# First products ahead of the second block's transposes, and roots by GpSimd's power operation

## The chip, the cores and the metric

The kernel runs on one core of one Trainium2 chip. The metric is the device time of one execution in microseconds (us). The engines are PE (TensorE, the matrix unit), DVE (VectorE), ACT (ScalarE), POOL (GpSimd) and SP (SyncE, which here only issues DMAs). Each engine works through its own queue in order: an instruction that waits for another engine holds all that stand behind it on its own engine.

## The reference, cut to what matters

The program computes one layer of a hybrid block for 16 learned meta tokens and 2048 tokens (T = 2064) of 1024 f32 values. What this change touches is the first product, `p`, and the norm ahead of it:

```python
def rms_norm(x, g):
    xf = x.astype(jnp.float32)
    y = xf * lax.rsqrt(jnp.mean(xf * xf, axis=-1, keepdims=True) + EPS)
    return (y * g.astype(jnp.float32)).astype(x.dtype)
...
h = jnp.concatenate([meta, x], axis=1)
p = rms_norm(h, norm_mix_pre[l]) @ w_in[l]
...
oa = rg_lru_group(xa, ya, ...)          # a recurrence over the tokens
ob = forgetting_attention_group(...)    # 8 heads with a forget gate
oc, v_own = rwkv7_group(pc, ...)        # a recurrence over the tokens
mixed = jnp.concatenate([oa, ob, oc], axis=-1) @ w_out[l]
h = h + rms_norm(mixed, norm_mix_post[l])
...
f = causal_dwconv(rms_norm(h, norm_ffn_pre[l]) @ ffn_up[l], ffn_conv[l])
f = (jax.nn.gelu(gate, approximate=True) * val) @ ffn_down[l]
h = h + rms_norm(f, norm_ffn_post[l])
```

The inputs of `oa`, `ob` and `oc` are columns of `p`.

## The kernel before, in words

**Number format.** The large products run on pairs: a value is split into a high and a low half, ACT copies the high half, DVE subtracts it from the value for the low one, and a product is three matmuls (high by high, low by high, high by low; L181 to L183).

**Stages.** The first stage is the input projection, with the two recurrences running beside it; attention, the output projection and the two feed-forward products follow. The change is in the first stage. It takes the tokens in thirds (`part` 0, 1, 2) of two blocks each (`w_in_tokens`): 400 tokens (the meta tokens and three tiles of 128) and 384, then 384 and 384, then 256 and 256.

**Tokens.** For each tile `w_in_norm` calls `norm_transpose`. SP loads the tile `xt` into one of four buffers `nt_x` (L131). ACT squares it and sums (L123). DVE makes the reciprocal root from the sum, by three small operations and three Newton steps of two (`rstd_from`, L98 and L99), and scales the tile by root and gain (L136). PE transposes it in eight pieces into two PSUM tiles `pst` (L149). ACT copies the high half `xh` (L155), and DVE makes the low half `xl` (L156). The transposes of all tiles of a third, of both blocks, are written ahead of that third's products.

**Products.** `w_in_part` is a generator. It begins with the forget gate's columns (`w_in_gate`: 16 matmuls a block, L300 and L301, into `psf`; ACT and DVE bring the result to `fo`, and SP stores it to DRAM as `scr_f`, L306). Then come 24 units of 128 columns each; a unit is 24 matmuls for each block, into `psp`. In the first third `w_in_weights` loads a unit's raw weights into a buffer of the token tiles (`nt_x`, L171), splits them on ACT (L175) and DVE (L176) into `wh` and `wl`, and stores both halves to DRAM for the other thirds, which only read them back.

**What stands around it.** Between the tokens and the first products, DVE zeroes a tile and POOL issues 12 DMAs of it into the padding of `scr_p` (L2202 to L2204). After the gate and the first 12 units (READY = 13, the gate counted as one) come the constants: attention's masks (`attn_consts`), those of the recurrences (`rwkv_consts`, `lru_consts`), and columns of parameters that PE transposes (L911, `pscol`). Then the recurrences run as generators beside the rest of the products. The forget gate's own chain (`gate_block`, L411 to L429) is one of their parts: SP reads `scr_f` back, and ACT and DVE take its logarithm and sums.

**What sets the order.** The program's text is not yet the order in the queues. A scheduler runs the program on a modelled timeline and deals the instructions to the engines' queues, with a priority by their place in the text; a changed text or a changed modelled duration deals what follows anew. `issue_after(x)` makes the instructions inside it wait for x, so that they aren't put early.

Names of the recurrence that will be met: `rps` are its PSUM tiles, L1203 its first products, L1252 (L1298 in the changed kernel) the matmuls of a small triangular solve, in which PE, ACT and DVE take turns; `rwitmp` (L1222, then L1268) are small products of that solve on POOL.

## Time and profile before

| What | Before |
|---|---|
| Median of 3 runs | 2978.02 us (2972.48, 2978.02, 2979.31) |
| The profiled execution's own time | 2974.88 us |
| Its span, first to last instruction | 2973.2 us |
| PE busy | 2840.2 us, 96% of the span |
| DVE, ACT, POOL busy | 2015.4, 1505.3, 1281.3 us |

The page cuts the span into 40 equal slices of 74 us and gives each engine's busy share in tenths, and under PEclk the TensorE clock that was granted, in tenths of full speed:

```profile
PE   6999999999978889999999999999999999999998
DVE  5257654675678766556756988888778787646766
POOL 1001121131214566766722667455655444656443
PEclk9999899999989899999999999999999999999999
```

PE is full but for the first slice and those around 850 us, where the first stage ends. In the clock's row the fifth slice (297 to 372 us) shows 8: there lies the passage from the first third to the second. The passage to the last third lies around 600 us, in the eighth and ninth, where the clock stays at 9 or more.

### The profile page before, as it was taken

The numbers are of one execution on the slowest core, as the hardware profiler recorded it, in microseconds if no ns is written. First come the engines' busy times: TensorE is split into PE (matmuls) and PEld (weight loads), VectorE is DVE, ScalarE is ACT, GpSimd is POOL, SyncE is SP. The second block draws the span as 40 slices with busy tenths as digits, with TensorE's granted clock in tenths as the row PEclk, the third lists the DMA queues.
The fourth block names the chain that finished last, engine by engine and source line by source line (L and its number), as shares of the span: only waits on it lengthen the run. The fifth ranks groups of instructions, "written<-read, shape, count | busy, mean of one in ns | idle before, by whom it ended". The sixth has DMA issues, their size and how long they took to land.

```text
span 2973.2 us, 53343 instructions
## 1 busy us (share of the span) xinstructions
PE 2840.2 (96%) x18854; PEld 2448.6 (82%) x18854; DVE 2015.4 (68%) x3974; ACT 1505.3 (51%) x2937; POOL 1281.3 (43%) x1555
## 2 busy tenths in 40 slices
PE   6999999999978889999999999999999999999998
PEld 6998899889865555566568999999999999787887
DVE  5257654675678766556756988888778787646766
ACT  4246432444346555445635665666575665324333
POOL 1001121131214566766722667455655444656443
PEclk9999899999989899999999999999999999999999
DMA  6776479576654257535245665577777774436453
GB/s 219 235 233 223 156 246 322 171 240 213 209 127 95 70 130 215 125 95 130 72 133 187 204 191 173 167 230 211 205 212 219 218 199 131 155 114 222 148 171 121
DMA packets 470344, 530.52 MB, mean 178 GB/s; under 512 B 86862, under 2 KB 356888, under 8 KB 468524
## 3 DMA queue, kind: packets, MB, share of 16 engines
q1 hardware_dynamic: 469308, 526.18, 58.4%
q8 instruction: 148, 2.42, 0.3%
q14 instruction: 120, 0.98, 0.1%
q0 software_dynamic: 768, 0.93, 0.1%
HBM read 368.07 MB, written 158.90 MB: 177 GB/s over the span
## 4 chain that ended last, share of the span: by engine, by line
PE 72%; DVE 8%; DMA 7%; ACT 5%; POOL 4%; issue 3%; SPq 1%; DVEq 0%; POOLq 0%; ACTq 0%
PE psu L181 9%; PE psu L182 9%; PE psu L183 9%; PE psp L183 5%; PE psp L182 5%; PE psp L181 5%; PE psd L181 4%; PE psd L182 4%; PE psd L183 4%; PE po L733 3%; PE sc L710 2%; PE pswo L181 2%; PE pswo L182 2%; PE pswo L183 2%; PE mx L581 2%
## 5 line engine op out<-in xcount | busy, mean ns | idle before, releaser
L182 PE MATMUL psu<-xo,uw 128*128 128x344 f32 x1848 | 591.5, 320 | 0.0
L181 PE MATMUL psu<-xo,uw 128*128 128x344 f32 x1848 | 586.0, 322 | 3.5 <-DVE vb L1907 2.1
L183 PE MATMUL psu<-xo,uw 128*128 128x344 f32 x1848 | 581.9, 320 | 0.3 <-DVE uw L1716 0.3
L181 PE MATMUL psp<-xh,wh 128*128 128x384 f32 (+2 forms) x1152 | 378.3, 328 | 0.1
L183 PE MATMUL psp<-xh,wl 128*128 128x384 f32 (+2 forms) x1152 | 377.0, 328 | 0.7 <-DMA wl<-scr_wk 0.7
L182 PE MATMUL psp<-xl,wh 128*128 128x384 f32 (+2 forms) x1152 | 377.6, 328 | 0.0
L1716 DVE TENSOR_TENSOR uw<-uq,uw 128x512 fp32r<-128x512 f32 x341 | 318.8, 940 | 61.3 <-ACT uw L1715 58.3
L181 PEld LDWEIGHTS psu<-xo,uw 128*128 128x128 f32 x1848 | 345.8, 188 | 5.1 <-DVE vb L1907 3.1
L182 PEld LDWEIGHTS psu<-xo,uw 128*128 128x128 f32 x1848 | 347.2, 188 | 0.0
L183 PEld LDWEIGHTS psu<-xo,uw 128*128 128x128 f32 x1848 | 345.7, 188 | 1.1 <-DVE uw L1716 1.1
L1715 ACT ACTIVATE uw<-uq 128x512 fp32r<-128x512 f32 x462 | 288.1, 627 | 100.1 <-PE psu L183 47.3
L715 ACT ACTIVATE p<-sc,bias 128x512 f32<-128x512 f32 (+4 forms) x352 | 196.4, 590 | 166.8 <-PE sc L711 141.9
L586 DVE TENSOR_REDUCE mc<-mx 128x1 f32<-128x512 f32 (+5 forms) x352 | 191.8, 566 | 119.4 <-PE mx L581 82.9
L1855 DVE SCALAR_TENSOR_TENSOR uy<-psu,ffn_cols,uy 128x342 f32<-128x342 f32 (+1 forms) x390 | 220.6, 567 | 62.4 <-ACT uy L1853 60.7
L1716 POOL TENSOR_TENSOR uw<-uq,uw 128x512 fp32r<-128x512 f32 x121 | 184.1, 1521 | 136.7 <-ACT uw L1715 112.9
L1863 POOL TENSOR_TENSOR uy<-uy,uy 128x342 f32<-128x342 f32 (+1 forms) x132 | 144.2, 1092 | 228.7 <-DVE uy L1855 63.1
L183 PEld LDWEIGHTS psp<-xh,wl 128*128 128x128 f32 x1152 | 219.9, 191 | 7.1 <-issue 4.6
L181 PEld LDWEIGHTS psp<-xh,wh 128*128 128x128 f32 x1152 | 219.8, 191 | 4.5 <-issue 2.6
L182 PEld LDWEIGHTS psp<-xl,wh 128*128 128x128 f32 x1152 | 220.0, 191 | 3.7 <-issue 2.3
L754 POOL TENSOR_TENSOR acc<-acc,p 128x512 f32<-128x512 f32 (+3 forms) x186 | 196.5, 1059 | 48.5 <-DVE acc L754 21.4
L1716 DVE TENSOR_TENSOR fo<-u,fo 128x896 fp32r<-128x896 f32 x88 | 100.3, 1140 | 133.0 <-ACT fo L1715 132.4
L1715 ACT ACTIVATE fo<-u 128x896 fp32r<-128x896 f32 x88 | 81.2, 923 | 207.6 <-PE psd L183 122.3
(489 smaller groups left out, 6301.5 us busy)
## 6 DMA issues: line engine op xcount, KB each, us to landing
uq<-scr_us SPq DMA_DIRECT2D x220, 256.0 KB
uq<-in_ffn_up_dram SPq DMA_DIRECT2D x209, 256.0 KB
wl<-scr_wk SPq DMA_DIRECT2D x48, 512.0 KB
wh<-scr_wk SPq DMA_DIRECT2D x48, 512.0 KB
u<-scr_ff SPq DMA_DIRECT2D x88, 256.0 KB
scr_ff<-uy SPq DMA_DIRECT2D x110, 171.0 KB
raw<-in_w_in_dram SPq DMA_DIRECT2D x24, 512.0 KB
scr_wk<-wh SPq DMA_DIRECT2D x24, 512.0 KB
```

Source lines behind the costliest of these rows:

```text
L181: nc.tensor.matmul(out, ah, bh, start=first, stop=False, skip_group_check=more)
L182: nc.tensor.matmul(out, ah, bl, start=False, stop=False, skip_group_check=more)
L183: nc.tensor.matmul(out, al, bh, start=False, stop=last, skip_group_check=more)
L581: nc.tensor.matmul(ps[:rows, : e - a], q3[:, qo : qo + rows], k2[:, a:e], start=True, stop=not last)
L586: self.reduced = nc.vector.tensor_reduce(mc[:rows, i, ci : ci + 1], ps[:rows, : e - a], axis=AX.X, op=ALU.max)
L715: last = nc.scalar.activation(p[:rows, :w], ps[:rows, :w], AF.Exp, bias=bias[:rows, j : j + 1])
L733: mm = nc.tensor.matmul(po[at : at + 64, c0:n], v1[:rows, j], p[:rows, : n - c0], start=start and i < 2, stop=end and i + 2 >= len(group), ...
L754: eng.tensor_tensor(a, ps_[0][0][:rows, c0:n] if start and i == 1 else a, p[:rows, : n - c0], op=ALU.add)
L1715: core.nc.scalar.activation(hi, src, AF.Copy)
L1716: (eng or core.nc.vector).tensor_tensor(lo, src, hi, op=ALU.subtract)
L1855: core.conved = stt(y[:, :n], src[:, i : n + i], cw[:, 44 * i + cc : 44 * i + cc + 1], y[:, :n], op0=ALU.mult, op1=ALU.add)
L1863: core.pooled = nc.gpsimd.tensor_tensor(v[:, :n], g[:, :n], v[:, :n], op=ALU.mult)
```

## The change

1. **Roots.** For the tokens of all three thirds the root is one POOL operation, `pow` with the exponent -0.5 from a constant tile `power` (128x1; new L128), after one DVE operation that makes the mean (new L127). The eight other small DVE operations of a tile are gone. After the last third's tokens `core.power` is cleared, and later norms are as before.
2. **Order in the first third.** `w_in_norm` leaves the three tiles of block 1 unturned. `w_in_part` writes the gate and the first unit of block 0, one tile of block 1, the second unit of block 0, the other two tiles, and then the gate and both units for block 1.
3. **Weights of the first two units.** They are loaded ahead of the first product into a buffer of their own, `rw_e` in a pool of the recurrence (`rp`), no longer into `nt_x`. The gate's weights of the first third lie in the pool `us`.
4. **What stood ahead.** The zeros and their 12 DMAs are written after the gate and the first 12 units, and wait for the last `pow` up to there (`core.powered`); so do attention's masks. The recurrences' constants and the columns wait for it too, and for the store of the fourth unit's weights (`begun`).

```diff
     core.nc.scalar.activation(junk, src, AF.Square, accum_out=ss)
+    if core.power is not None:
+        ms, y = v[:, 0:1], v[:, 2:3]
+        core.nc.vector.tensor_scalar(ms, ss, 1.0 / width, EPS, op0=ALU.mult, op1=ALU.add)
+        core.powered = core.nc.gpsimd.tensor_tensor(y, ms, core.power[: ms.shape[0], :], op=ALU.pow)
+        return y
     return rstd_from(core.nc, v, ss, width, core.apart)
...
-    for t0, n, tl, hi, lo in blocks:
-        for s, rows in tl:
-            src = meta if s < META else x[s - META : s - META + rows, :]
-            late = part == 1 and (s, rows) not in blocks[0][2][:2]
-            after = (lambda: core.tc.issue_after(core.rounded.ins)) if late else nullcontext
-            norm_transpose(core, pools, psum, src, rows, gain, [(hi, lo, s - t0, 0, rows)], after)
+    def tile(block, s, rows):
+        t0, _, _, hi, lo = block
+        src = meta if s < META else x[s - META : s - META + rows, :]
+        late = part == 1 and (s, rows) not in blocks[0][2][:2]
+        after = (lambda: core.tc.issue_after(core.rounded.ins)) if late else nullcontext
+        norm_transpose(core, pools, psum, src, rows, gain, [(hi, lo, s - t0, 0, rows)], after)
+    core.unturned = []
+    for block in blocks:
+        for s, rows in block[2]:
+            if part == 0 and block is blocks[1]:
+                core.unturned.append((block, s, rows))
+            else:
+                tile(block, s, rows)
+    core.turn_tile = lambda: tile(*core.unturned.pop(0))
     return blocks
...
-def w_in_weights(core, pools, w_in, c0, scr, part):
-    if part == 0:
-        src = w_in[:, c0 : c0 + P].rearrange("(k p) c -> p k c", p=P)
+def w_in_weights(core, pools, w_in, c0, scr, part, raw=None):
+    src = w_in[:, c0 : c0 + P].rearrange("(k p) c -> p k c", p=P)
+    if raw is not None:
+        pair = hi, lo = [pools["w"].tile([P, KD, P], F32R, tag=s, name=core.n(s)) for s in ("wh", "wl")]
+        core.loaded = core.nc.sync.dma_start(raw, src)
+        core.rounded = core.nc.scalar.activation(hi[:], raw, AF.Copy)
+        core.nc.vector.tensor_tensor(lo[:], raw, hi[:], op=ALU.subtract)
+    elif part == 0:
         pair = split_load(core, pools["w"], (pools["nt"], "nt_x", None), src, [P, KD, P], "w")
     else:
         core.turns += part == 2
...
-    w = pools["w"].tile([P, KD, P], F32R, tag="wh", name=core.n("fw"))
+    home, tag = ("w", "wh") if part else ("us", "us")
+    w = pools[home].tile([P, KD, P], F32R, tag=tag, name=core.n("fw"))
     flat, kept = w[:].rearrange("p k c -> p (k c)").bitcast(F32), w_in_kept(scr, 3 * D)[0]
     if part == 0:
         raw = pools["st"].tile([P, KD, 8], F32, tag="stv", name=core.n("fraw"))
...
         nc.sync.dma_start(kept, flat)
     else:
         nc.sync.dma_start(flat, kept)
-    for t0, n, tl, hi, lo in blocks:
+    def products(t0, n, tl, hi, lo):
         ps = psum.tile([P, 512], F32, tag="mm", name=core.n("psf"))
         for k in range(KD):
             nc.tensor.matmul(ps[:, :n], w[:, k], hi[:, k], start=k == 0, stop=False)
...
         o = pools["st"].tile([8, 400], F32, tag="stl", name=core.n("fo"))
         nc.vector.tensor_tensor(o[:, :n], ps[0:8, :n], a[:, :n], op=ALU.add)
         nc.sync.dma_start(scr["f"][:, t0 : t0 + n], o[:, :n])
-    yield False
-    yield True
+    return products
 def w_in_part(core, pools, psum, w_in, blocks, scr, part):
-    yield from w_in_gate(core, pools, psum, w_in, blocks, scr, part)
+    gate = w_in_gate(core, pools, psum, w_in, blocks, scr, part)
...
+    if part == 0:
+        raws = pools["rp"].tile([P, 2, KD, P], F32, tag="rw_e", name=core.n("raw"))
+        firsts = [
+            (w_in_weights(core, pools, w_in, c0, scr, part, raws[:, i]), kind, c0)
+            for i, (kind, c0) in enumerate(units[:2])
+        ]
+        for i, block in enumerate(blocks):
+            gate(*block)
+            yield i > 0
+            for w, kind, c0 in firsts:
+                step(w, block, kind, c0)
+                if i == 0:
+                    core.turn_tile()
+                yield i > 0
+            while core.unturned:
+                core.turn_tile()
+        del units[:2]
+    else:
+        for block in blocks:
+            gate(*block)
+        yield False
+        yield True
     for kind, c0 in units[:-2]:
         w = w_in_weights(core, pools, w_in, c0, scr, part)
...
             ps_mm = pool(p1a, "ps_mm", 5, space=PSUM)
-            sums = up_sums(core, pool(p1a, "us", 1), a["ffn_up"], scr, EARLY)
+            pools["us"], pools["rp"] = pool(p1a, "us", 1), rp
+            sums = up_sums(core, pools["us"], a["ffn_up"], scr, EARLY)
+            core.power = core.const.tile([P, 1], F32, name="power")
+            nc.vector.memset(core.power[:], -0.5)
             following = w_in_norm(core, pools, ps_mm, x, meta, g_pre, 0)
             for part in range(3):
                 blocks = following
+                units = w_in_part(core, pools, ps_mm, a["w_in"], blocks, scr, part)
+                for i in range(READY if part == 0 else 0):
+                    while not next(units):
+                        pass
+                    if i == 4:
+                        begun = core.loaded.ins
                 if part == 0:
                     zeros = pools["st"].tile([P, PAD], F32, tag="sth", name="zeros")
                     nc.vector.memset(zeros[:], 0.0)
                     for r in range(0, A_ROWS + C_ROWS, P):
-                        nc.gpsimd.dma_start(scr["p"][r : r + P, 0:PAD], zeros[:])
-                units = w_in_part(core, pools, ps_mm, a["w_in"], blocks, scr, part)
-                for _ in range(READY if part == 0 else 0):
-                    while not next(units):
-                        pass
-                if part == 0:
-                    attn_consts(core)
+                        with tc.issue_after(core.powered.ins):
+                            nc.gpsimd.dma_start(scr["p"][r : r + P, 0:PAD], zeros[:])
+                    with tc.issue_after(core.powered.ins):
+                        attn_consts(core)
                     shared, core.const = core.const, rc
+                    p1c = ExitStack()
+                    p1c.enter_context(tc.issue_after(begun))
+                    p1c.enter_context(tc.issue_after(core.powered.ins))
                     rk = rwkv_consts(
                         core, gp, ps_ae,
                         {
...
                     )
                     columns(core, gp, ps_ae, [a["ffn_conv"].rearrange("i (r p) -> (i r) p", p=P)], "", cw)
+                    p1c.close()
                     R = Rwkv(core, rp, dp, ps_rw, ps_ae, scr, rk)
...
                 if part < 2:
                     following = w_in_norm(core, pools, ps_mm, x, meta, g_pre, part + 1)
+                else:
+                    core.power = None
```

The three places in the engines' queues (the numbers in names are running ones):

**PE, the opening.** Before, from the last tile of block 0 (`xt_220`) on; `xt_249`, `xt_278` and `xt_307` are the tiles of block 1, L911 are transposed columns, and L300 is the first product (the gate):

```order
L149 MATMUL pst_242<-ident,xt_220 128x128 x4
L911 MATMUL pscol_1309<-ident,rows_1307 128x128
L149 MATMUL pst_264<-ident,xt_249 128x128 x4
L149 MATMUL pst_271<-ident,xt_249 128x128 x4
L911 MATMUL pscol_1314<-ident,rows_1312 128x4
L149 MATMUL pst_293<-ident,xt_278 128x128 x4
L149 MATMUL pst_300<-ident,xt_278 128x128 x4
L149 MATMUL pst_322<-ident,xt_307 128x128 x4
L149 MATMUL pst_329<-ident,xt_307 128x128 x4
L300 MATMUL psf_357<-xh_129,fw_350 128x400
L301 MATMUL psf_357<-xl_130,fw_350 128x400
```

In the changed kernel, from block 0's last tile (`xt_201`) on; L155 is now the transpose, L323 and L324 the gate, L187 to L189 the units:

```order
L155 MATMUL pst_209<-ident,xt_201 128x128 x4
L155 MATMUL pst_216<-ident,xt_201 128x128 x4
L323 MATMUL psf_245<-xh_131,fw_223 128x400
L187 MATMUL psp_267<-xh_131,wh_231 128x400
L324 MATMUL psf_245<-xl_132,fw_223 128x400
L323 MATMUL psf_245<-xh_131,fw_223 128x400
```

and from the end of the first unit of block 0, with block 1's first tile (`xt_295`):

```order
L187 MATMUL psp_267<-xh_131,wh_231 128x400
L188 MATMUL psp_267<-xl_132,wh_231 128x400
L189 MATMUL psp_267<-xh_131,wl_232 128x400
L155 MATMUL pst_303<-ident,xt_295 128x128 x4
L155 MATMUL pst_310<-ident,xt_295 128x128 x4
L187 MATMUL psp_317<-xh_131,wh_238 128x400
L188 MATMUL psp_317<-xl_132,wh_238 128x400
```

Block 0's products now follow its own last tile at once; block 1's first tile stands behind the gate and the first unit of block 0, its other two tiles behind the second unit, and the column transposes have left the opening.

**ACT, the same place of the changed kernel.** The gate's copy (L326), the first unit's result (L58), the copies of block 1's first tile (L161, from `pst_303` and `pst_310`), the forget gate's chain (L459 to L475, with a table load), and the copies of block 1's last two tiles (from `pst_353` on):

```order
L326 ACTIVATE fa_262<-psf_245 8x400
L58 ACTIVATE stp_292<-psp_267 128x400
L161 ACTIVATE xh_133<-pst_303 128x4x128
L161 ACTIVATE xh_133<-pst_310 128x4x128
L459 ACTIVATE rwr_1343<-rwk_1341,fb 8x400
L460 ACTIVATE rwr_1343<-rwr_1343 8x400
L461 ACT_TABLE_LOAD
L461 ACTIVATE rwr_1343<-rwr_1343 8x400
L475 ACTIVATE rwk_1352<-rwsq_1349 8x400
L161 ACTIVATE xh_133<-pst_353 128x4x128
L161 ACTIVATE xh_133<-pst_360 128x4x128
L161 ACTIVATE xh_133<-pst_375 128x4x128
```

Before, the gate's products, and so its chain, came behind the transposes and copies of both blocks.

**PE and DVE, the passage from the first third to the second.** PE before: `xt_3257` and `xt_3286` are the second third's last two tiles, L1252 to L1307 the solve and what follows it, L300 the second third's first product:

```order
L1252 MATMUL rps_2558<-rwxu_2339,rwsc_1644 32x32 x16
L1252 MATMUL rps_2623<-rwxf_2387,rwxu_2339 32x32
L1083 MATMUL eps_3380<-rwwa_3361,wa_up 128x256 x2
L1252 MATMUL rps_2623<-rwxf_2387,rwxu_2339 32x32 x15
L1296 MATMUL rps_2642<-rww_199_1645,rwsc_1644 64x64 x16
L149 MATMUL pst_3272<-ident,xt_3257 128x128 x4
L149 MATMUL pst_3279<-ident,xt_3257 128x128 x4
L1083 MATMUL eps_3386<-rwwa_3361,wa_up 128x256 x2
L1307 MATMUL rps_2693<-rww_199_1645,rwxf_2387 64x128
L149 MATMUL pst_3301<-ident,xt_3286 128x128 x4
L149 MATMUL pst_3308<-ident,xt_3286 128x128 x4
L300 MATMUL psf_3317<-xh_3137,fw_3315 128x384
```

PE in the changed kernel, with the same two tiles as `xt_3181` and `xt_3203`, and the recurrence's first products as L1213 and L1218:

```order
L1218 MATMUL rps_2136<-rwrav_2076,rwbk_2083 64x128 x2
L1213 MATMUL rps_2135<-rwrav_2076,rwbk_2083 128x128
L1218 MATMUL rps_2136<-rwrav_2076,rwbk_2083 64x128 x2
L1190 MATMUL eps_2093<-rwsq_1991,bones 128x512
L155 MATMUL pst_3189<-ident,xt_3181 128x128 x4
L155 MATMUL pst_3196<-ident,xt_3181 128x128 x4
L155 MATMUL pst_3211<-ident,xt_3203 128x128 x4
L155 MATMUL pst_3218<-ident,xt_3203 128x128 x4
L323 MATMUL psf_3227<-xh_3089,fw_3225 128x384
L324 MATMUL psf_3227<-xl_3090,fw_3225 128x384
L1213 MATMUL rps_2151<-rwrav_2076,rwbk_2083 128x128 x2
```

DVE before, where the Newton steps (L98, L99) of the two tiles stand between operations of the recurrences (L1282 is the solve's):

```order
L1223 TENSOR_REDUCE rwix_2303<-rwitmp_2306 128x8
L1282 COPY rwxu_2339<-rps_2558 32x256 x2
L99 SCALAR_TENSOR_TENSOR rs_3260<-rs_3260 128x1
L98 SCALAR_TENSOR_TENSOR rs_3289<-rs_3289 128x1
L1507 SCALAR_TENSOR_TENSOR rwlg_3072<-rwlg_3072,rwlu_3070 128x256
L1223 TENSOR_REDUCE rwix_2303<-rwitmp_2306 128x8
L1506 SCALAR_TENSOR_TENSOR rwlr_3071<-rwlr_3071,rwla_3073 128x256
L136 SCALAR_TENSOR_TENSOR xt_3257<-xt_3257,rs_3260,g_pre 128x1024
```

DVE in the changed kernel, with the differences of the tile before (L162), the means (L127) and the scalings (L142):

```order
L162 TENSOR_TENSOR xl_3090<-pst_3152,xh_3089 128x4x128
L162 TENSOR_TENSOR xl_3092<-pst_3167,xh_3091 128x4x128
L162 TENSOR_TENSOR xl_3092<-pst_3174,xh_3091 128x4x128
L1181 SCALAR_TENSOR_TENSOR rwbk_2083<-rwe_1979 128x8x64
L1098 SCALAR_TENSOR_TENSOR rwk_3282<-rwraw_3283,rwkv_cols,rwk_3282 128x256
L1188 SCALAR_TENSOR_TENSOR rwsq_1991<-rwsq_1991,rwkv_cols,rwr_2069 128x256 x2
L1098 SCALAR_TENSOR_TENSOR rwk_3282<-rwraw_3283,rwkv_cols,rwk_3282 128x256
L127 TENSOR_SCALAR rs_3184<-rs_3184 128x1
L127 TENSOR_SCALAR rs_3206<-rs_3206 128x1
L142 SCALAR_TENSOR_TENSOR xt_3181<-xt_3181,rs_3184,g_pre 128x1024
L142 SCALAR_TENSOR_TENSOR xt_3203<-xt_3203,rs_3206,g_pre 128x1024
L1222 TENSOR_TENSOR rwsc_2133<-rps_2135,rmask 128x4x128
```

Before, the solve stood ahead of the last two tiles' transposes; now both tiles stand ahead of it, and their scalings on DVE follow the tile before and some operations of the recurrence (L1098, L1181, L1188).

1 line of the change is left out of this document (added).

## The prediction, made before the run

> **What bounds the kernel now.** I read the busy times by stretch first, then the waits of PE, then the timeline of the opening. The stretches (start and end in us; then the length, and for each engine busy us and instructions; granted clock of PE; share of the DMA engines; GB/s):
>
> ```profile
> 0.00:36.60 36.60, 13.10 (x60) 10.83 (x61) 29.26 (x143) 16.47 (x32) 11.94 (x32) 1.00 0.66 204
> 36.60:281.00 244.40, 244.40 (x1400) 233.30 (x1399) 118.23 (x269) 99.34 (x181) 10.47 (x19) 1.00 0.71 231
> 281.00:316.70 35.70, 25.66 (x363) 21.52 (x361) 31.31 (x87) 27.61 (x56) 10.11 (x20) 0.62 0.38 120
> 316.70:560.00 243.30, 241.02 (x2058) 223.79 (x2057) 123.25 (x300) 87.31 (x169) 49.09 (x77) 1.00 0.75 249
> 560.00:620.00 60.00, 55.89 (x520) 49.42 (x520) 46.32 (x138) 28.39 (x58) 8.31 (x11) 1.00 0.60 197
> ```
>
> PE (first figure after the length) never rests from 36.6 to 281 us, in the products of the first third. So what this change can give lies in two holes: the opening, where PE works 13.1 of 36.6 us, and the passage from the first third to the second (281 to 316.7), where it idles 10.0 us and its clock is cut to 0.62. DVE (third figure) is the busiest engine in both, with 29.3 and 31.3 us. Who ended PE's waits in the two holes (us in total, times, longest):
>
> ```profile
> PE pst L149 <- DVE rs L99: 10.4, 1, 10.4
> PE pst L149 <- DVE lruv L1456: 4.5, 1, 4.5
> PE pst L149 <- DVE xt L136: 3.5, 2, 2.7
> ...
> PE rps L1252 <- DVE rwxu L1282: 4.5, 1, 4.5
> PE rps L1252 <- ACT rwsc L1205: 3.7, 1, 3.7
> ```
>
> The first three are the opening: transposes that wait for normalised tiles, and DVE gives them late because it computes roots and constants in between. The other two are the passage: PE's queue holds the recurrence's solve (L1252) ahead of the last two tiles' transposes, with no product to fill in.
>
> **The opening now, and its prices.** Timeline rows (start, duration, engine, line):
>
> ```profile
> 7.19 1.06 ACT L123 ACTIVATE xj<-xt 128x1024 bf16<-128x1024 f32 x1 [0.41 <-DMA xt<-in_x_dram]
> 10.73 1.06 ACT L123 ACTIVATE xj<-xt 128x1024 bf16<-128x1024 f32 x1 [0.42 <-DMA xt<-in_x_dram]
> 13.82 1.97 PE L149 MATMUL pst<-ident,xt 128*128 128x128 f32 x8 [0.78 <-DVE xt L136]
> 24.88 0.38 SPq L171 DMA_DIRECT2D raw<-in_w_in_dram  x1
> 28.85 1.06 ACT L175 ACTIVATE wh<-raw 128x1024 fp32r<-128x1024 f32 x1 [0.42 <-DMA raw<-in_w_in_dram]
> 33.45 3.42 PE L149 MATMUL pst<-ident,xt 128*128 128x128 f32 x16 [4.51 <-DVE lruv L1456]
> 39.43 0.34 PE L301 MATMUL psf<-xl,fw 128*128 128x400 f32 x1
> 39.61 0.34 PE L300 MATMUL psf<-xh,fw 128*128 128x384 f32 x1
> 280.32 0.93 PE L149 MATMUL pst<-ident,xt 128*128 128x128 f32 x7
> ```
>
> Block 0's last square starts at 10.73, so its data are there by then; the first products start only at 36.6. A matmul of 400 columns takes 0.18 us (39.43 to 39.61), one of 384 some 0.175. A tile's eight transposes take 1.97 us here, but 0.13 each at 280 us, so PE starts at half pace, and the dense 3.42 us at 33.45 bring it to full pace. (The clock column reads 1.00 there all the same.)
>
> The group view of the opening (count, then busy us and mean ns, then idle before):
>
> ```profile
> L136 DVE SCALAR_TENSOR_TENSOR xt<-xt,rs,g_pre 128x1024 f32<-128x1024 f32 x6 | 7.6, 1275 | 0.0
> L156 DVE TENSOR_TENSOR xl<-pst,xh 128x512 fp32r<-128x512 f32 x10 | 6.8, 684 | 0.1
> L98 DVE SCALAR_TENSOR_TENSOR rs<-rs 128x1 f32<-128x1 f32 x18 | 3.7, 216 | 0.0
> L99 DVE SCALAR_TENSOR_TENSOR rs<-rs 128x1 f32<-128x1 f32 x18 | 2.7, 158 | 0.0
> L176 DVE TENSOR_TENSOR wl<-raw,wh 128x1024 fp32r<-128x1024 f32 x1 | 1.2, 1226 | 0.3 <-ACT wh L175 0.3
> L155 ACT ACTIVATE xh<-pst 128x512 fp32r<-128x512 f32 x12 | 6.7, 589 | 6.4 <-PE pst L149 6.4
> ```
>
> **The power operation.** It takes eight small DVE operations from each of 17 tiles; the six Newton steps alone are 3 x 216 + 3 x 158 = 1.12 us a tile. It adds one GpSimd operation on 128x1. No row shows that function. The nearest are small GpSimd operations, the farthest its 128x512 form:
>
> ```profile
> L95 POOL TENSOR_SCALAR rs<-rs 128x1 f32<-128x1 f32 x21 | 7.6, 363 | 9.7 <-DVE rs L92 8.9
> L1222 POOL TENSOR_TENSOR rwitmp<-rwix,rwia 128x16 f32<-128x16 f32 x8 | 2.2, 270 | 125.7 <-DVE rwia L1217 125.7
> L1761 POOL TENSOR_TENSOR ds<-ds,ds 128x512 f32<-128x512 f32 x40 | 64.2, 1607 | 0.0
> L2204 POOL DMA_DIRECT2D scr_p<-zeros x12 | 6.6, 556 | 3.1 <-DMA scr_p<-zeros 2.9 <-DVE zeros L2202 0.3
> ```
>
> I take 0.35 us, by the first two; the ends are 0.27 and 1.6. (The last row is used further on.) The wait that it adds: GpSimd stands until the square and its scaling are done, and behind it stand GpSimd's mask constants, the zeroing DMAs and, in later thirds, the recurrence's small products (rwitmp), for which DVE and then PE wait.
>
> **The new opening, by these rows.** After the last square of block 0 (ends 11.9) ACT still has two weight copies (2.1), six tile copies (3.5), the square of the next tile (1.25) and small ones: done at about 19. DVE has two scalings (2.6), two weight differences (2.5), six tile differences (4.1): done at about 21. The weights: one load took 3.97 us (24.88 to 28.85); here two stand behind 2.1 MB, and at the 204 GB/s of the opening all 3.1 MB are in by 15 to 17, ahead of that. So products run densely from S = 21 (19 to 25) instead of 36.6.
>
> From S: block 0's gate and first unit, 40 x 0.18 = 7.2; half pace for the first 3.4 us costs 1.7; a tile's transposes 1.0; the second unit 24 x 0.18 = 4.3; two tiles' transposes 2.1. That ends at 37.3. Then a **new wait**: ACT holds the forget gate's chain ahead of the last two tiles' copies. That chain now:
>
> ```profile
> 40.93 0.30 SPq L306 DMA_DIRECT2D scr_f<-fo  x1
> 43.26 0.30 SPq L411 DMA_DIRECT2D rwk<-scr_f  x1
> 44.84 0.63 ACT L413 ACTIVATE rwr<-rwk,fb 8x400 f32<-8x400 f32 x1
> 46.06 1.28 ACT L415 ACT_TABLE_LOAD   x1
> 49.60 0.54 ACT L429 ACTIVATE rwk<-rwsq 8x400 fp32r<-8x400 f32 x1 [1.17 <-DVE rwsq L424]
> ```
>
> It takes 9.2 us from the store to L429's end, less 0.5 for a copy in between. The gate's products end at S + 7, the store goes out about 29.1, the chain is done at 37.8, four tile copies (2.4) and a difference (0.7) follow: PE goes on at about 41, after 3.7 us of idleness. The 64 products of block 1 (64 x 0.175 = 11.2) end at 52.2. Now the same work ends at 36.6 + 64 x 0.18 + 64 x 0.175 = 59.3. The column transposes, four small ones, move among the products and cost 0.6 at full pace. Gain of the opening: 59.3 - 52.2 - 0.6 = **6.5 us**. If S is 25 it is 2.5; without the new wait at S = 19 it is 12. The columns' loads, 12 zeroing DMAs and constants go later, beside products that fill PE to 281; were that cover gone, the 12 issues would cost 6.6 us of GpSimd (L2204).
>
> By the Trainium skill, TensorE: Matmul & The Clock Gate, Part 1: The HAM clock gate, an idle stretch of about 3.4 us halves PE's clock and as long a busy one restores it. The trace agrees for the start (3.42 us of transposes, then full pace) but not at 301 to 316, where the slow time lasts longer. By that rule the 3.7 us wait would cost 1.7 more, and the opening would give 4.8 instead of 6.5.
>
> **The passage.** Its rows now:
>
> ```profile
> 287.29 1.05 SPq L131 DMA_DIRECT2D xt<-in_x_dram  x2
> 292.48 1.04 ACT L123 ACTIVATE xj<-xt 128x1024 bf16<-128x1024 f32 x1
> 302.44 1.43 DVE L136 SCALAR_TENSOR_TENSOR xt<-xt,rs,g_pre 128x1024 f32<-128x1024 f32 x1
> 306.11 1.97 PE L149 MATMUL pst<-ident,xt 128*128 128x128 f32 x8
> 310.62 1.75 PE L149 MATMUL pst<-ident,xt 128*128 128x128 f32 x7
> ```
>
> The last two tiles are squared at 292.5 and transposed at 306 and 310.6, since their Newton steps alternate on DVE with the solve. Lost: 10.0 us idle, and at a clock of 0.62 up to 25.66 x 0.38 = 9.7 more; I count 18.5. In the changed order the two scalings stand on DVE behind eight differences (5.5) and some eight recurrence operations (about 4.6, at a mean of 0.57: below the 0.68 of the 128x512 differences), ahead of the solve. So the transposes can run some 12.5 us after the last product, while PE has 7.7 us of transposes and recurrence products until then. That leaves about 5 us idle and 4 at half pace, and the solve then lies among products. I add 1 for waits of the solve there: **gain 8.5 us**; the ends are nothing (the loads, not DVE, set it) and 13. The passage to the last third (560 to 620) loses 4.1 us now and holds its order nearly: nothing, give or take 3.
>
> **Sum.** 6.5 + 8.5 = 15.0. The profiled execution took 2974.9 us, a span of 2973.2 and 1.7 around it; it is 3.1 below the median of 2978.0. So 2959.9 for such an execution, and 2963 for the median.
>
> **Rivals.**
> - *Only the opening gains.* The last two tiles' loads wait in SP's queue behind stores, and land while other loads press; now they take 5.2 us from issue to square, more than the Newton steps' excess in a good order. Then PE waits as long as now: 2978 - 6.5 = 2971.5. For it: the passage follows from rows that a scheduler dealt anew; against: 10 us lie between square and scaling.
> - *Slower: a dear power operation holds GpSimd's queue.* At a price p, four in a row set S once 4p passes the slack: S = 11.4 + 4p, and the two of the passage move its transposes by 2p behind the solve's operations. At p = 4 the gains are used up. At p = 6 the opening loses 7, the passage gains nothing, and the last third's four tiles, for whose scalings PE waits likewise, cost some 8: 2993. For it: no row shows the function. Against: all GpSimd rows of that size are under 0.4.
> - *A slow first use only.* If the first power operation alone comes late by 5 us (some four loads like ACT's 1.28 us table), S moves by the 3 to 4 that ACT and DVE do not hide: 2967. The Trainium skill, GPSIMD Engine Reference, Instruction dispatch, says that the first call of freshly loaded code pays about 6 us; by that, 2968. No first use on GpSimd shows such a gap here.
> - *More.* The new wait and the idle of the passage both vanish: 12 + 13: 2953.
>
> **How the numbers follow.** Forecast 0.48 (own range 2957 to 2970), only the opening 0.25, dear power 0.11, slow first use 0.06, more 0.10. A measurement of this kernel tells about 0.2%, 6 us, from no change. Below 2972 lie the forecast, more, most of the slow first use and half of the second: 0.73 faster; 0.17 within; 0.10 slower. Range 2955 to 2978: it leaves out the slower case and the far end of the last.
>
> **What would show it.** Power rows of 0.27 to 0.4 us; first product at 19 to 22 us; PE idle 3 to 4 us near 37 to 41, ended by ACT's tile copies; the recurrence's L1252 (then L1298) among products; under 10 us lost between the thirds. Wrong if the power rows pass 1.6 us, if the first products wait for weights past 25, or if the passage still shows a clock near 0.6.

## The result

The changed kernel takes 2959.45 us (median of 6 runs, 2954.59 to 2962.62), the kernel before 2977.95 (6 runs, 2972.48 to 2983.33): a ratio of 0.9931, interval 0.9918 to 0.9944. The forecast was 2963 with a range of 2955 to 2978. The first profile of the change is of the execution that took 2962.62 us, with a span of 2960.9; each kernel was profiled a second time. Two slow executions are left out of the ratios given here, one of 9562.87 us (power operation alone) and one of 3113.85 us (weights through the token buffers). Where the stages stand in the two profiles of each kernel (us from the span's start; the third unit is the third of the 24 units of columns):

| Point | Before | Changed |
|---|---|---|
| First product | 36.6, 36.8 | 18.4, 18.5 |
| First product of the third unit | 59.6, 60.3 | 51.8, 54.8 |
| Last product of the first third | 280.1, 282.1 | 267.1, 269.7 |
| First product of the second third | 312.2, 313.7 | 288.8, 290.4 |
| First product of the last third | 612.5, 614.9 | 603.6, 603.3 |
| Last product of the projection | 865.1, 869.4 | 856.5, 855.1 |
| First product of the output projection | 1182.7, 1188.2 | 1168.7, 1164.6 |
| Span | 2973.2, 2978.2 | 2960.9, 2957.0 |

The stretches of the changed kernel up to the last third, in its first profile (start and end; length, then busy us and instructions of PE, its weight loads, DVE, ACT, POOL; granted clock; DMA share; GB/s):

```profile
0.00:20.17 20.17, 7.15 (x34) 5.51 (x34) 15.52 (x52) 12.91 (x23) 3.98 (x13) 0.96 0.89 271
20.17:51.77 31.60, 29.70 (x150) 28.87 (x151) 14.11 (x22) 12.57 (x22) 4.44 (x14) 0.86 0.51 166
51.77:267.30 215.53, 214.69 (x1210) 205.36 (x1210) 97.47 (x221) 82.92 (x154) 18.57 (x35) 0.99 0.73 236
267.30:288.80 21.50, 14.70 (x80) 10.50 (x78) 19.22 (x40) 11.93 (x24) 5.94 (x6) 0.68 0.79 271
```

In the first row PE still works only 7.15 of 20.17 us; in the second it is full but for 1.9 us, at a clock of 0.86; the fourth is the passage, still with 6.8 us idle and a clock of 0.68. The waits of PE behind these holes (us in total, times, longest):

```profile
PE pst L155 <- DVE xt L142: 9.1, 2, 8.9
PE rps L1213 <- DVE rwbk L1181: 6.5, 1, 6.5
PE psf L323 <- ACT xh L161: 3.2, 2, 1.9
```

The first is the first tile, the second the passage, the third holds the forecast new wait (1.9 of its 3.2 us). The timeline shows it, and the price of the power operation:

```profile
6.94 0.57 POOL L128 TENSOR_TENSOR rs<-rs,power 16x1 f32<-16x1 f32 x1 [5.09 <-DVE rs L127]
20.67 0.54 PE L323 MATMUL psf<-xh,fw 128*128 128x400 f32 x1
25.34 0.42 PE L189 MATMUL psp<-xh,wl 128*128 128x400 f32 x1
38.63 0.44 PE L323 MATMUL psf<-xh,fw 128*128 128x384 f32 x1 [1.87 <-ACT xh L161]
42.62 0.34 PE L189 MATMUL psp<-xh,wl 128*128 128x384 f32 x1
```

The first power operation takes 0.57 us. Products run densely from 20.2 us, at half pace until 25.3; PE waits 1.87 us at 36.8 (3.65 in the second profile) and is at half pace again to 42.6. The granted clock (third figure from the end) shows the same two stretches:

```profile
18.70:25.50 6.80, 6.18 (x18) 5.56 (x18) 5.69 (x10) 2.40 (x5) 2.65 (x6) 0.50 1.05 389
39.20:42.60 3.40, 3.38 (x11) 3.00 (x10) 0.95 (x2) 0.00 (x0) 0.00 (x0) 0.50 1.06 270
```

Two places must be compared with care. At 267 us the changed kernel has done 64 of the recurrence's matmuls on `rps` (8.82 us) where the kernel before, at 280, had done 112 (14.66 us); with those on `eps`, other tiles of the recurrence (12.24 and 14.10 us), 7.7 us of PE have moved into the second third. At the last third's first product the two stand nearly equal (1622 matmuls on `rps`, and 1616 before). The account up to there: 10.3 us gained on the mean of the two profiles, some 5 in the opening and the first third (12.7 less the 7.7 moved), some 5 in the passage and the second third. A further 7.4 us (mean of the two profiles) comes behind the projection, where attention begins beside the rest of the recurrences. The second profile of the kernel before shows a granted clock of 0.964, the other three 0.976 to 0.980; against the first one alone the two gains are 8.9 to 9.1 and 5.4 to 8.1 us. The stretch behind the projection:

```profile
865.40:1182.70 317.30, 59.31 (x1246) 0.90 0.52 129
```

```profile
856.80:1168.70 311.90, 55.97 (x1184) 0.87 0.53 131
```

These are the matmuls on `rps` from the projection's end to the first product of the output projection, before and after, each with the length of the stretch first: 62 fewer are left in the changed kernel, and the stretch is 5.4 us shorter (the second profiles: 318.5 and 309.2).

### The profile page after: what moved, and what is told of

Its sections match the earlier page's. It is cut to its first block, busy times and chain, and to the rows that moved or that the text cites. A ratio compares the mean times of both kernels' runs of the same rounds, so it can differ in the third digit from the quotient of the medians.

```text
span 2960.9 us, 53225 instructions
## 1 busy us (share of the span) xinstructions
PE 2844.5 (96%) x18854; PEld 2448.4 (83%) x18854; DVE 2002.2 (68%) x3839; ACT 1505.8 (51%) x2937; POOL 1297.3 (44%) x1572
## 4 chain that ended last, share of the span: by engine, by line
PE 69%; DVE 7%; ACT 6%; DMA 5%; issue 2%; POOL 2%; SPq 1%; DVEq 0%; ACTq 0%; POOLq 0%
PE psu L187 9%; PE psu L188 9%; PE psu L189 9%; PE po L779 4%; PE psd L187 4%; PE psd L188 4%; PE psd L189 4%; PE psp L187 2%; PE psp L189 2%; PE psp L188 2%; PE sc L756 2%; PE mx L627 2%; PE sc L757 2%; PE pswo L187 2%; PE pswo L188 2%
## 5 line engine op out<-in xcount | busy, mean ns | idle before, releaser
L187 PE MATMUL psu<-xo,uw 128*128 128x344 f32 x1848 | 585.8, 322 | 3.3 <-ACT u L1933 2.3
L189 PE MATMUL psu<-xo,uw 128*128 128x344 f32 x1848 | 582.0, 320 | 0.3 <-DVE uw L1762 0.2
L187 PE MATMUL psp<-xh,wh 128*128 128x384 f32 (+2 forms) x1152 | 383.0, 333 | 0.4 <-DVE rww L1462 0.3
L189 PE MATMUL psp<-xh,wl 128*128 128x384 f32 (+2 forms) x1152 | 375.6, 326 | 0.0
L1762 DVE TENSOR_TENSOR uw<-uq,uw 128x512 fp32r<-128x512 f32 x341 | 319.0, 940 | 60.6 <-ACT uw L1761 57.5
L187 PEld LDWEIGHTS psu<-xo,uw 128*128 128x128 f32 x1848 | 345.8, 188 | 4.8 <-ACT u L1933 2.6
L189 PEld LDWEIGHTS psu<-xo,uw 128*128 128x128 f32 x1848 | 345.7, 188 | 1.2 <-DVE uw L1762 1.1
L187 PEld LDWEIGHTS psp<-xh,wh 128*128 128x128 f32 x1152 | 220.4, 191 | 7.7 <-issue 4.4
L189 PEld LDWEIGHTS psp<-xh,wl 128*128 128x128 f32 x1152 | 220.3, 191 | 4.3 <-issue 3.0
L800 POOL TENSOR_TENSOR acc<-acc,p 128x512 f32<-128x512 f32 (+3 forms) x186 | 196.4, 1059 | 49.8 <-DVE acc L800 22.2
```

What stands on the lines that cost most here:

```text
L187: nc.tensor.matmul(out, ah, bh, start=first, stop=False, skip_group_check=more)
L189: nc.tensor.matmul(out, al, bh, start=False, stop=last, skip_group_check=more)
L800: eng.tensor_tensor(a, ps_[0][0][:rows, c0:n] if start and i == 1 else a, p[:rows, : n - c0], op=ALU.add)
L1762: (eng or core.nc.vector).tensor_tensor(lo, src, hi, op=ALU.subtract)
```

## The experiments

The kernel before was measured anew beside each group of kernels, with medians of 2975.45 to 2976.59 us where the result has 2977.95. So ratios to it compare kernels better than medians do; the changed kernel's is 0.9931. An edit can also change the scheduler's order far from its place; each kernel is therefore compared by stages too, and has one profile.

**The parts of the change.** One kernel keeps the order and takes Newton's steps for all roots, with a GpSimd copy of each root for what waits for `core.powered`; one takes the power operation alone; two use it in some thirds only.

```diff
+    if core.newton:
+        y = rstd_from(core.nc, v, ss, width, core.apart)
+        core.powered = core.nc.gpsimd.tensor_copy(v[:, 5:6], y)
+        return y
     if core.power is not None:
```

> The change without its roots: Newton's steps on DVE in all thirds, and a POOL copy of each root so that POOL still waits at the same place. Theory A (the prediction's: the shorter roots make the passage to the second third): the opening keeps some 4 of its gain, since four tiles' Newton steps, 1.1 us of DVE each, push the first products from 18.4 to about 22 us; the passage gains nothing: about 2974. Theory B (the later start of the recurrences takes the solve out of the passage, whatever makes the roots): the passage keeps its gain, the last product of the first third ends 3 to 4 us later than in the changed kernel, and the time is about 2963.

Measured: 2974.02 us, ratio to before 0.9996 (0.9981 to 1.001). The first product came at 24.3, the third unit at 58.2; the passage took 26.8 us, the second third to the last third's first product 319.0. Neither theory holds whole: the time is that of A, but the solve has left the passage, as B has it.

The second is the kernel before with the new branch of `rstd_of`:

> The kernel before with the power operation for the roots of all three thirds and nothing else. In the opening, first products at about 33 instead of 36.6 us (the Newton steps of the last tiles are gone; weights still come through the token buffers). Theory A: the passage gains its 8: about 2967. Theory B: the solve stays in the passage, PE still idles over 5 us there at a clock near 0.6 to 0.7: about 2974.

Measured: 2990.87 us, ratio 1.0051 (1.0031 to 1.0071): slower than the kernel before and the changed one, and than both theories. Its GpSimd queue:

```profile
1.52 4.56 POOL L2212 DMA_DIRECT2D scr_p<-zeros  x8
7.56 0.54 POOL L2212 DMA_DIRECT2D scr_p<-zeros  x1 [1.47 <-DMA scr_p<-zeros]
9.14 1.73 POOL L2212 DMA_DIRECT2D scr_p<-zeros  x3 [1.04 <-DMA scr_p<-zeros]
11.69 1.09 POOL L128 TENSOR_TENSOR rs<-rs,power 16x1 f32<-16x1 f32 x2
```

The first root waits for the zeroing DMAs until 11.69 us, and then DVE works through the recurrences' constants before it scales a tile; the first product comes at 37.8. The passage is shorter, 23.1 us instead of 32.1 and 31.6, but still holds the solve; 66 of its matmuls on `rps` have moved behind it, and the second third takes 310.3 us instead of 300.2. From the first third's last product to the last third's first it is 333.4 us, as before (332.4 and 332.8): the shorter roots alone gain nothing there, as theory B has it. Eleven us more than in the changed kernel went in attention (456 us from the output projection's first product, at 1181.6, to the feed-forward's first, against 445), whose order the scheduler dealt anew.

> The change with the power operation in the first third only, Newton's steps in the second and the last. Opening as in the changed kernel (first product at 18.4 us). Theory A: the passage loses its 8: about 2968. Theory B: the passage keeps its order and its gain: within 2 us of the changed kernel, about 2960.

Measured: 2972.78 us (0.9994; 0.998 to 1.0008). Opening as in the changed kernel (18.1, third unit at 51.5); the passage takes 26.2 us instead of 21.7, the second third to the last third's first product 318.5 instead of 314.8, and attention again had another order (453 us). The time fits neither theory; the stages up to the last third (7.4 us later) fit A.

> The change with Newton's steps in the first third and the power operation in the other two. Both theories: the passage as in the changed kernel; the opening loses 3 to 4 (first products at about 22 us): 2963. If the power operation is worth nothing in the opening (weights or ACT set the first product), about 2960.

Measured: 2962.98 us (0.9959; 0.9944 to 0.9974); first product 24.8, third unit 60.3, passage 22.1, second third 312.8. That is the expected time, with a larger loss in the opening than expected.

Together: with the order as changed, the power operation in the first third brings the third unit 6.7 us forward (58.2 without it to 51.5 with it; the changed kernel itself stands at 51.8 and 54.8 in its two profiles), and in the others it takes 4.5 us out of the passage (26.8 to 22.1, 26.2 to 21.7) and 4 to 6 out of the second third. The order alone, and the power operation alone, gain nothing. In all three kernels with the late constants the solve stood behind the passage, with Newton's steps too: it is not the shorter roots that move it.

**What left the opening.** The zeros go back ahead of `w_in_part`, and masks and constants lose their `issue_after` (`...` marks lines left out).

```diff
+                if part == 0:
+                    zeros = pools["st"].tile([P, PAD], F32, tag="sth", name="zeros")
+                    nc.vector.memset(zeros[:], 0.0)
+                    for r in range(0, A_ROWS + C_ROWS, P):
+                        nc.gpsimd.dma_start(scr["p"][r : r + P, 0:PAD], zeros[:])
                 units = w_in_part(core, pools, ps_mm, a["w_in"], blocks, scr, part)
...
-                    with tc.issue_after(core.powered.ins):
-                        attn_consts(core)
+                    attn_consts(core)
...
-                    p1c.enter_context(tc.issue_after(begun))
-                    p1c.enter_context(tc.issue_after(core.powered.ins))
```

> The change with the zeroing DMAs, the masks and the constants back where they stood, ahead of the first products and with no issue_after. Theory (moving them is what lets the power operation pay, as the kernel with the power operation alone suggests): the first power operation waits behind the zeroing DMAs to about 11.7 us instead of 6.9, the first product comes at about 24 instead of 18.4 us, and the solve stands in the passage again: the last third's first product at about 611 us instead of 603.6. Rival (they cost nothing): 18.4 and 604. Its attention has the other of two orders that the scheduler deals, which took 8 to 11 us more in two kernels so far, so the whole is about 2978 by the theory, 2969 by the rival.

Measured: 2975.86 us (0.9995; 0.9986 to 1.0005): all of the gain is gone. The timeline of PE:

```profile
15.34 0.27 PE L957 MATMUL pscol<-ident,rows 22*128 22x22 f32 x1 [15.34 <-DMA rows<-in_rwkv_ln_b_dram]
19.05 1.03 PE L155 MATMUL pst<-ident,xt 16*128 16x16 f32 x8 [3.44 <-DVE xt L142]
20.25 4.63 PE L155 MATMUL pst<-ident,xt 128*128 128x128 f32 x24 [0.17 <-DVE xt L142]
```

PE stands until 15.34 us for the rows of a column transpose, which its queue holds ahead of every tile. The first root came at 10.80 us, the first product at 26.9, the solve was in the passage again, and the last third began at 614.4: the theory held, with the opening later than it said. Attention took no longer (443.8 us), and in that stretch PE's order is the changed kernel's row for row; the expected other order, with its 8 to 11 us, did not come.

**The order that names the change.** Block 1's tiles go ahead of all products again; everything else stays.

```diff
+LATE_TURN = False
...
-            if part == 0 and block is blocks[1]:
+            if part == 0 and block is blocks[1] and LATE_TURN:
...
-                if i == 0:
+                if i == 0 and core.unturned:
                     core.turn_tile()
```

> The change with block 1's three tiles turned first again, ahead of all products (so without the part that gave the change its name); weights beside the tiles, the power operation and the late constants stay, and the order from the passage on is the changed kernel's row for row. Theory (the products of block 0 hide the tiles of block 1): the first product waits for all seven tiles, some 30 us by DVE's work (7 scalings, 12 differences, 2 weight differences from 7.5 us on), and the first third ends 6 to 8 us later: about 2966. Rival (the half clock behind a short wait and the wait itself give it back: 2.4 + 1.9 + 1.9 us in the changed kernel): first products at 28, dense and at full clock, the first third ends within 2 us of the changed kernel's 267: about 2960.

Measured: 2960.11 us (0.9945; 0.9926 to 0.9964), the same as the changed kernel within the intervals. Its timeline and a stretch:

```profile
21.62 4.87 PE L155 MATMUL pst<-ident,xt 128*128 128x128 f32 x24 [4.87 <-DVE xt L142]
26.79 0.42 PE L326 MATMUL psf<-xh,fw 128*128 128x400 f32 x1 [0.30 <-DVE fw L318]
27.05 0.34 PE L327 MATMUL psf<-xl,fw 128*128 128x400 f32 x1
```

```profile
26.80:36.60 9.80, 9.80 (x54) 9.80 (x55) 2.62 (x5) 3.49 (x6) 0.71 (x4) 1.00 0.59 185
```

The products begin 8.4 us later, but behind 4.87 us of dense transposes they run at full pace from the start, with no hole: the third unit begins at 49.8, against 51.8 and 54.8. The rival held: products ahead of the tiles give back in half pace and in the new wait what they gain. By this one profile they even cost something: the first third's last product comes at 263.4 (267.1 and 269.7 in the changed kernel) and the last third's first at 598.9 (603.6 and 603.3). The medians don't show those 4 to 5 us, and the profile is of this kernel's shortest execution, 2950.28 us.

**Weights beside the tiles**, undone:

```diff
-        raws = pools["rp"].tile([P, 2, KD, P], F32, tag="rw_e", name=core.n("raw"))
-            (w_in_weights(core, pools, w_in, c0, scr, part, raws[:, i]), kind, c0)
+            (w_in_weights(core, pools, w_in, c0, scr, part), kind, c0)
```

> The change with the first two units' weights loaded through the token buffers nt_x again instead of a buffer of their own. Theory (the buffer of their own brings the weights early): the loads wait until tiles of block 0 are turned, the first unit's weights land at about 17 instead of 12.5 us; first dense products at 22 to 23 instead of 20; end of the first third 2 to 4 us later. Rival: 20 and 267 as in the changed kernel, ACT and DVE set it. Its order from the second third on is dealt anew, so only the end of the first third tells.

Measured: 2968.23 us (0.9974; 0.996 to 0.9989). Its profile is of the execution of 3113.85 us, at a granted clock of 0.842, so its stages can't be compared; in its first 20 us, where the clock still was 0.98, the weight copies came at 14.87 and 17.85 us (12.49 and 14.13 in the changed kernel), and the products were dense from 20.8 instead of 20.2. That is less than either expected, and less than a microsecond there does not make 9 in all; its later order differs, and what the buffer is worth stays open.

**The price of the power operation:** two in a row for each root, the first with the exponent 1 (`core.unit`).

```diff
+        core.nc.gpsimd.tensor_tensor(y, ms, core.unit[: ms.shape[0], :], op=ALU.pow)
-        core.powered = core.nc.gpsimd.tensor_tensor(y, ms, core.power[: ms.shape[0], :], op=ALU.pow)
+        core.powered = core.nc.gpsimd.tensor_tensor(y, y, core.power[: ms.shape[0], :], op=ALU.pow)
```

> The change with two power operations in a row for each root (exponents 1 and -0.5), so that each root costs 0.55 us more on GpSimd, in the same place. If the price lies on the chain (the prediction's rival of a dear power operation, S = 11.4 + 4p): four in a row move the first product from 18.4 to about 20.5, the passage to the second third grows by about 1, that to the last by 1 to 2: about 2964. If GpSimd has slack in all three places: unchanged, about 2960.

Measured: 2970.18 us (0.998; 0.997 to 0.999), 10.7 more than the changed kernel by the medians, 14.6 by the ratios, for 0.55 us a tile. The opening, where PE's order stayed the same, lost nothing in the end: first product at 19.7, 1.3 later, third unit at 50.8. The passage:

```profile
267.60:297.90 30.30, 21.20 (x107) 15.03 (x106) 24.33 (x50) 12.63 (x25) 5.76 (x8) 0.67 0.66 214
```

It takes 30.3 us: with one more operation in the program the scheduler dealt the passage anew, with 27 more of PE's instructions in it (the recurrences' matmuls, mostly at half pace). So this measures an order more than a price. Its new wait tells something else:

```profile
35.25 1.91 PE L156 MATMUL pst<-ident,xt 128*128 128x128 f32 x16
38.99 0.44 PE L324 MATMUL psf<-xh,fw 128*128 128x384 f32 x1 [1.83 <-ACT xh L162]
40.24 0.33 PE L324 MATMUL psf<-xh,fw 128*128 128x384 f32 x1
40.41 0.34 PE L325 MATMUL psf<-xl,fw 128*128 128x384 f32 x1
```

Behind the same 1.91 us of transposes PE waits 1.83 us, as good as the 1.87 of the changed kernel, and then runs at full pace (0.17 us from product to product). So the length of the wait alone does not settle whether half pace follows.

**The new wait**, taken away by putting the first block's forget chain behind block 1's last copy (`core.copied`) and difference (`core.turned`):

```diff
-        gate_block(core, R, f_bias, scr, blk[2])
+        with ExitStack() as es:
+            if part == 0 and blk is blocks[0]:
+                for ins in (core.copied, core.turned):
+                    es.enter_context(core.tc.issue_after(ins.ins))
+            gate_block(core, R, f_bias, scr, blk[2])
```

> The change with the forget gate's chain of the first block put behind the copies and differences of block 1's tiles on ACT and DVE; PE's order is the same, row for row. Theory (the new wait costs what it shows): PE's wait of 1.9 us at 36.8 us and the half clock behind it, 38.6 to 42.3 us, go: 3.5 us faster than the changed kernel, about 2956. Rival (the first third's PE time is not what ends the stage, the recurrence's work on DVE is): the wait goes, and the passage waits longer by the same: about 2959.5.

Measured: 2950.71 us (0.991; 0.9893 to 0.9928). In its timeline the wait has shrunk, and with it the half pace:

```profile
36.72 0.44 PE L323 MATMUL psf<-xh,fw 128*128 128x384 f32 x1 [0.35 <-ACT xh L161]
37.95 0.33 PE L323 MATMUL psf<-xh,fw 128*128 128x384 f32 x1
38.12 0.34 PE L324 MATMUL psf<-xl,fw 128*128 128x384 f32 x1
```

The third unit begins at 48.5 (3.3 and 6.3 us earlier than in the two profiles of the changed kernel), the last third at 599.7 (3.7 to 4 earlier). PE's order is the changed kernel's from the first row to the last, so this comparison is the cleanest here. By its stages the theory held; the median fell by 8.7 and the ratio by 6.3 us' worth, with intervals that overlap slightly, and the stages show about half of that.

**The passage**, treated like the opening, on top of that: block 0's first two units ahead of block 1's tiles, the gate behind them.

```diff
-            if part == 0 and block is blocks[1]:
+            if part < 2 and block is blocks[1]:
...
+            firsts = [(w_in_weights(core, pools, w_in, c0, scr, part), kind, c0) for kind, c0 in units[:2]]
+            for i, block in enumerate(blocks):
+                for w, kind, c0 in firsts:
+                    step(w, block, kind, c0)
+                    if i == 0:
+                        core.turn_tile()
+                    yield i > 0
+                while core.unturned:
+                    core.turn_tile()
...
+        gate = gate or w_in_gate(core, pools, psum, w_in, blocks, scr, part)
```

> The kernel with the forget gate's chain moved, and in the second third too: first two units of block 0 ahead of block 1's tiles, the gate behind these units. Theory (the passage to the second third is lost for want of products that may run, not for want of DVE or loads): from the last product of the first third to the first of the second 21.7 us fall to about 8, PE's wait of 6.5 us is filled: 8 to 10 us faster than the changed kernel with the gate moved: about 2947. Rival (DVE or the token loads bound the passage): block 0's products run early, then wait for block 1's tiles as long as before: about 2955.

Measured: 2945.84 us, ratio 0.9898 (0.9883 to 0.9913): the fastest kernel here. The stretch behind the first third's products:

```profile
261.30:282.00 20.70, 18.59 (x121) 15.43 (x120) 18.10 (x37) 11.10 (x23) 4.86 (x6) 1.00 0.79 268
```

PE works 18.59 of 20.7 us at full clock, where the changed kernel had 14.70 of 21.5 at 0.68. The last third begins at 594.4, 5.3 us earlier than with the gate alone. So the theory held in kind: with products that may run, PE hardly rests in the passage. The gain is some 5 us instead of the 8 to 10 expected.

**Second profiles** of the two kernels, in the table above:

> The kernel before, unchanged, for a second profile: if the stretch from the first third's last product to the last third's first repeats within 2 us (332.4 us in the first profile) and that from the last unit of the projection to the first product of the output projection (317.6) comes shorter, the part of the difference between the two medians that the two profiles do not show lies in that second stretch.

> The changed kernel, unchanged, for a second profile, whose first one was the slowest of its six runs: the stages up to the last third (603.6 us) repeat within 2 us, and the 3 to 8 us that it is faster by lie in attention, where its clock was lowest.

Measured: 2979.91 and 2958.71 us. In the kernel before, the stretch between the thirds repeated (332.8 us), and so did the one behind the projection (318.8, not shorter). In the changed kernel 603.3 repeated, but not the stages ahead of it: the third unit came 3.0 and the first third's last product 2.6 us later than in the first profile, so one profile tells the opening no better than that. Behind the projection both profiles of the changed kernel are shorter than both of the kernel before.

Yet that stretch, from the last product of the projection to the first of the output projection, takes 308.3 to 314.4 us in nine other kernels (all but the one profiled at a clock of 0.842), against 317.6 and 318.8 before: 309.1 with the power operation alone, 309.3 with the order alone, and neither of these two was faster as a whole. So this gain is not tied to one part of the change; whether any new order would bring it is not shown.

## Why the prediction was right, and where its steps were not

- **The sum** was 15.0; the medians differ by 18.5. Up to the last third, where all its terms lie, 10.3 were gained, about 5 for each term instead of 6.5 and 8.5. The rest came behind the projection, where the prediction had no term. That the total came so near the forecast is luck; the 10.3 alone would have given about 2968, still within the range.
- **The opening, 6.5:** the third unit's first product came 7.8 and 5.5 us earlier, the new wait was 1.87 and 3.65 us (forecast 3.7, by the same chain on ACT), dense products began at 20.2 (forecast 21). The size is about right and its owner is not: the prediction let it follow from products that run from 21 instead of 36.6 us. With all tiles first they ran from 26.8 and ended no later, so that this part of the reasoning was right in its number by luck; with the constants in front, or with Newton's steps, the gain was gone (third unit at 61.0 and 58.2). The step that failed is the count of what the column transposes, zeros and constants cost: 6.6 us "were that cover gone"; putting them all back cost 16.4 by the medians, 19 by the ratios, the solve's place in the passage included.
- **The clock:** behind 1.87 us of waiting PE ran at half pace from 38.63 to 42.6; the 3.40 us at a clock of 0.50 are 1.7 us lost, which the sum had left out (in the second profile 5.93 us at 0.50 behind a wait of 3.65, about 3 lost). The half pace at the start lasted from 20.2 to 25.3, some 2.4 us lost instead of 1.7. By the Trainium skill (TensorE: Matmul & The Clock Gate, Part 1: The HAM clock gate) an idle stretch of about 3.4 us halves the clock, and the prediction's estimate by it was 1.7 more for the wait. The size agrees, but the wait that was followed by half pace was only 1.87 us long, and one of 1.83 us in the kernel with two power operations was followed by full pace; what decides between the two is not shown.
- **The power operation** takes 0.55 us in the median (mean 0.64, one of 1.54), not 0.35, within the bounds of 0.27 and 1.6. No first use was late (0.57 us like the rest), so the 6 us for the first call of freshly loaded code (the Trainium skill, GPSIMD Engine Reference, Instruction dispatch) don't show here, and the rival of a slow first use falls.
- **The dear power operation** as a rival fell: the price is 0.55. Its break-even of 4 us was not reached by any run; twice the price cost nothing in the opening, and what it cost elsewhere came with another order.
- **The passage, 8.5:** the prediction left 9 us lost; 6.8 idle and 14.70 x 0.32 = 4.7 at half clock, 11.5 in all, were. So of the 18.5 us that the prediction counted as lost there, 7 were gained, of which the solve's new place and the moved work took some back. That DVE's shorter chain does it holds for 4 to 5 us, and only with the late constants; that the solve leaves the passage is due to these, for it stayed in both kernels that lack them. With the passage gaining, the rival "only the opening gains" fell; "more" did not come, though the kernels with the gate's chain moved show that both holes could be closed further. The loads, the "nothing" end of that term, come close to binding, as rows of the changed kernel show:

```profile
274.36 1.28 SPq L137 DMA_DIRECT2D xt<-in_x_dram  x2
278.71 0.79 PE L1213 MATMUL rps<-rwrav,rwbk 64*128 64x128 f32 x2 [6.54 <-DVE rwbk L1181]
280.04 1.06 ACT L124 ACTIVATE xj<-xt 128x1024 bf16<-128x1024 f32 x1 [3.78 <-DMA xt<-in_x_dram]
285.94 3.08 PE L155 MATMUL pst<-ident,xt 128*128 128x128 f32 x16
```

The last two tiles are issued at 274.36 and squared only from 280.04, after ACT waited 3.78 us for them; their transposes follow at 285.94. But what ended PE's 6.54 us of idleness was DVE's `rwbk`, and from there PE worked without a gap up to these transposes. So no row shows that the loads cost time.

- **The signs:** the solve among products came, and so did a wait ended by ACT's tile copies. Not met were power rows of 0.27 to 0.4 us and under 10 us lost between the thirds (11.5); and the clock of 0.68 in the passage is not far from the 0.6 that was to show the prediction wrong.

- **Not foreseen:** some 7 us behind the projection. That 62 matmuls of the recurrence less are left there is shown; why the last third took up more of them is not, nor that they are the cause: kernels that gained nothing as a whole have the shorter stretch too. The cause stays open.

## What to carry to other kernels

Before products are pulled ahead of other work, ask whether the work that is already dense would run at full clock: eight microseconds of earlier products at half pace with a hole in them were worth nothing, and with the hole closed the third unit came only 1.3 us earlier than with all tiles first (48.5 and 49.8). An operation on an in-order queue costs what stands ahead of it: the power operation was slower with the zeroing DMAs ahead of it, and paid only with these and the constants behind it. Where a scheduler deals the order, undo each part of a change by itself and compare stages at equal work done, since an edit in one place can move others by as much as it gains.

## What the runs showed that was not expected

- Behind 1.91 us of transposes and 1.87 us of waiting, PE lost its full clock for 3.4 us; behind 1.91 and 1.83 us, in another kernel, it kept it. Behind 4.87 us of dense transposes it had it at once.
- The order of attention that the scheduler dealt in two kernels (power operation alone, and in the first third only) took 453 to 456 us instead of 443 to 446, in stages that no edit touched.
